# Prompt attention: the scores of two heads as products of 64 rows on the two halves of TensorE, with queries of both heads in one tile

## The chip, the cores and the metric

The kernel runs on one core of a Trainium2 chip. The metric is the device time of one execution in microseconds (us), the median of several runs. One further execution was recorded by the hardware profiler; all rows below come from it.

## The reference, cut to what matters

The program is one step of a two-layer decoder trunk: a gated DeltaNet layer, then a layer of dilated window attention, each with a feed-forward block, over a prompt of 1024 rows and 64 decode rows. The change lies in the prompt's attention of the second layer. There are 3 head groups of 16 heads of 64 channels, and 4 K/V heads, each shared by 4 query heads of a group. For every group (window, dilation) in (128, 1), (512, 4), (2048, 16) the reference does, on blocks of 128 queries against at most 256 keys:

```python
qr = residues(q).reshape(b, dil, nb, B_BLOCK, nkv, qpk, dh)
kw = key_windows(k)
vw = key_windows(v)
bias = -slope[:, :, None, None] * (dil * delta).astype(np.float32)
scores = jnp.einsum('brnqgpd,brnkgd->brngpqk', qr, kw, preferred_element_type=jnp.float32) * (dh ** -0.5) + bias
scores = jnp.where(valid[:, None, None], scores, -jnp.inf)
lse = jax.nn.logsumexp(scores, axis=-1)
probs = jnp.exp(scores - lse[..., None])
out = jnp.einsum('brngpqk,brnkgd->brnqgpd', probs, vw.astype(jnp.float32))
```

The queries are `h @ w_q`, and all of it is wanted in float32.

## The kernel before

All large products are made of float32 values split in two parts that TensorE takes in its one-pass form of float32 (`F32R` in the code): a high part, and a low part that holds the rest. A full product is then hi·hi + lo·hi + hi·lo.

The attention of the prompt runs over 24 units: 4 K/V heads, 3 groups, 2 pairs of heads. `attn_prompt` lets three kinds of generators take turns (`merge`): `q_proj` makes the queries of the next unit, `attend` works on the current one, and `combine` merges the groups of a K/V head that is done. The tile scheduler of the language sets the final order on each engine; between engines there are only semaphores, and each engine takes its instructions in order.

`q_proj` (L1366) is 72 products a unit: 3 chunks of 384, 352 and 352 rows, each 8 slices of the model by 3 parts. A chunk is then taken out of its PSUM bank (L1376, L1377). For each of the two heads of the unit ScalarE writes the high part, scaled, to partitions 0 to 63 of the head's own tile `qs[a]`, and VectorE the low part to partitions 64 to 127 of the same tile. So a column of `qs[a]` is hi over lo, and the K tiles `kh` and `kl` hold the 64 channels of K twice, on both halves of the partitions.

`attend` pushes 8 blocks a unit through a pipeline of five stages, one push a block. `scores` makes the scores of a block; two stages later `flip` turns the probabilities (transposes on TensorE, L1470, taken out by ScalarE, L1473, and VectorE, L1474), and two later `outputs` multiplies them with V (L1489) and, every second block, takes the result out (L1506 on ScalarE, L1504 on VectorE).

The scores of a block are 4 products of 128 rows (L1451). For each head `qs[a]` is multiplied with `kh`, which gives hi·kh + lo·kh at once, and then with `kl`. Both heads lie in one PSUM bank. VectorE then adds the bias and finds the maximum, an operation a head (L1455), and ScalarE takes the exponential (L1457). A block has 256 keys, or 128 at the edge of a residue class and in the whole third group.

The 8 PSUM banks of the stage are dealt out by `self.banks(mm=2, sc=2, tr=2, o=2)`: two each for `q_proj`, the scores, the transposes and the outputs.

Of the kernel before, what the change touches and what calls it, by code (L numbers as in the profile page):

```python
# [13 lines left out]
F32 = mybir.dt.float32  # L14
F32R = mybir.dt.float32r
BF16 = mybir.dt.bfloat16
AF = mybir.ActivationFunctionType
ALU = mybir.AluOpType
# [4 lines left out]
P = 128  # L23
D = 1024
KD = D // P
SP = 1024
# [38 lines left out]
def stream(*stages):  # L65

    live = [None] * len(stages)

    def push(item):
        live.insert(0, None if item is None else [item, None])  # L70
        live.pop()
        for s, x in zip(stages, live):
            if x is not None:
                x[1] = s(x[0], x[1])
            yield
    return push
# [1175 lines left out]
G = 3  # L1252
# [3 lines left out]
SLOPE = [[2.0 ** (-8.0 * (g * 16 + h + 1) / 48) for h in range(16)] for g in range(G)]  # L1256
# [25 lines left out]
class Attn:  # L1282
# [37 lines left out]
    def attn_prompt(self, ap, bp, h, w_q, kv, qd, st, oT):  # L1320

        nc = self.nc
        dist = bp.tile([P, G, 256], F32, name="dist", bufs=1)
        for g, d in ((0, 1), (1, 4)):
            nc.gpsimd.iota(dist[:, g], pattern=[[d, 256]], base=-d * P, channel_multiplier=-d, allow_small_or_imprecise_dtypes=True)
            nc.gpsimd.affine_select(out=dist[:, g], in_=dist[:, g], pattern=[[-1, 256]], base=P, channel_multiplier=1,
                                    compare_op=ALU.is_ge, fill=-FAR)
            nc.gpsimd.affine_select(out=dist[:, g], in_=dist[:, g], pattern=[[1, 256]], base=0, channel_multiplier=-1,
                                    compare_op=ALU.is_ge, fill=-FAR)
        d2 = dist[:, 2, :P]  # L1330
        nc.gpsimd.iota(d2, pattern=[[16, P]], base=0, channel_multiplier=-16, allow_small_or_imprecise_dtypes=True)
        nc.gpsimd.affine_select(out=d2, in_=d2, pattern=[[-1, P]], base=0, channel_multiplier=1, compare_op=ALU.is_ge, fill=-FAR)
        nc.gpsimd.affine_select(out=d2.rearrange("p (c i) -> p c i", c=2), in_=d2.rearrange("p (c i) -> p c i", c=2),
                                pattern=[[64, 2], [0, 64]], base=63, channel_multiplier=-1, compare_op=ALU.is_ge, fill=-FAR)
        units = [(kv_, g, pr) for kv_ in range(NKV) for g in range(G) for pr in range(2)]
        v = {"spread": (ap.tile([P, 4, DH], F32R, name="cheads", bufs=1), ap.tile([P, 8], F32, name="cblk", bufs=1), ap.tile([P, G, P], F32R, name="cws", bufs=1))}
        n = len(units)
        push = stream(*(partial(f, ap=ap, bp=bp, v=v, st=st) for f in (self.scores, self.rest, self.flip, self.rest, self.outputs)))
        for i in range(n + 2):
            ts = []  # L1340
            if i < n:
                ts.append(self.q_proj(units[i], bp, v, h, w_q, qd))
            if i == 2:
                self.spread_rows(ap, *v["spread"])
            if 0 < i <= n:
                ts.append(self.attend(units[i - 1], push, bp, v, kv, dist, i == n))
            if i > 1 and i % 6 == 1:
                last = self.combine(units[i - 2][0], ap, v, oT, st)
                ts += [last] if i < n else []
            merge(*ts)  # L1350
        return last

    def q_proj(self, u, bp, v, h, w_q, qd):
        nc = self.nc
        kv_, g, pr = u
        hi, lo = h[:2]
        col = g * 1024 + (kv_ * 4 + pr * 2) * DH
        w = self.wtile(w_q[:, col:col + P].rearrange("(k p) c -> p k c", p=P), [P, KD, P], gain=self.gain[:, 4], eng=nc.gpsimd)
        d = DIL[g]
        qs = [bp.tile([P, SP], F32R, tag=f"qs{a}", name="qs") for a in range(2)]  # L1360
        for n0, n in CHUNKS:
            ps = self.bank("mm")
            i = 0
            for k in range(KD):
                for a, b in ((w[0], hi), (w[0], lo), (w[1], hi)):
                    nc.tensor.matmul(ps[:, :n], a[:, k, :], b[:, k, n0:n0 + n], start=i == 0, stop=i == 23)  # L1366
                    i += 1
                yield 1 / 24
            a1 = min(n0 + n, SP) - n0
            for a in range(2):  # L1370
                src = ps[64 * a:64 * a + 64, :a1].rearrange("p (i r) -> p i r", r=d)

                def dst(rows):
                    return qs[a][rows].rearrange("p (r i) -> p i r", r=d)[:, n0 // d:(n0 + a1) // d, :]
                c = 0.125 / SLOPE[g][kv_ * 4 + pr * 2 + a]
                nc.scalar.activation(dst(slice(0, 64)), src, AF.Copy, scale=c)  # L1376
                nc.vector.scalar_tensor_tensor(dst(slice(64, 128)), src, c, dst(slice(0, 64)), op0=ALU.mult, op1=ALU.subtract)  # L1377
            if n0 + n > SP:
                t = bp.tile([P, SD], F32, name="qdt")
                nc.scalar.activation(t, ps[:, a1:n], AF.Copy, scale=0.125)  # L1380
                at = ((g * NKV + kv_) * 2 + pr) * SD
                nc.sync.dma_start(qd[:, at:at + SD], t)
        v[u] = qs
# [57 lines left out]
    def scores(self, i, _, ap, bp, v, st):  # L1441

        nc = self.nc
        ((kv_, g, pr), qs, (kh, kl, vh), dist, stat), b = i
        kb, nk = self.span(g, b)
        n = nk * P
        bo = P if (nk == 1 and g < 2) else 0
        ps = self.bank("sc").rearrange("p (a k) -> p a k", a=2)
        for a in range(2):
            for j, k in enumerate((kh, kl)):  # L1450
                nc.tensor.matmul(ps[:, a, :n], qs[a][:, b * P:(b + 1) * P], k[:, kb * P:kb * P + n], start=j == 0, stop=j == 1)  # L1451
        s = bp.tile([P, 2, 256], F32, name="s", bufs=4)
        for a in range(2):
            m = stat[:, 0, a, b:b + 1]
            nc.vector.tensor_tensor_reduce(out=s[:, a, :n], in0=ps[:, a, :n], in1=dist[:, g, bo:bo + n], scale=-SLOPE[g][kv_ * 4 + pr * 2 + a],  # L1455
                                           scalar=FAR, op0=ALU.add, op1=ALU.min, accum_out=m)
            nc.scalar.activation(s[:, a, :n], s[:, a, :n], AF.Exp, bias=m, scale=-1.0, accum_out=stat[:, 1, a, b:b + 1])  # L1457
        return s
# [262 lines left out]
class Trunk(Net, Gdn, Attn):  # L1721
    def run(self, a, dbias, outs):
# [63 lines left out]
        with ExitStack() as eh:  # L1786
            h2 = []
            with ExitStack() as ef:
                self.fast = []
                self.fast_pool(ef)  # L1790
                with em as es:
                    mixer = self.mixer_out(self.mixer_pool(es), mw, oT, (0, 1), x0, x1, fast((0, 2)), late=True)
                    next(mixer)
                    self.weights(es, 3, 1)
                    self.banks(mm=4, sm=4)
                    merge(mixer)
                with ExitStack() as es:
                    self.fast_pool(ef)
                    self.banks(mm=6, sm=2)
                    self.ffn_in(a["ffn_w_in"][0], gs, gd)  # L1800
            kv = dram("kv", [T, NKV, 3, DH])
            qd = dram("qd", [P, G * NKV * 2 * SD])
            flat = lambda t: t.rearrange("b t k d -> (b t) (k d)")
            kv_outs = [flat(t) for t in (kcp, vcp, kcs, vcs)]
            def after():
                self.h_pool(eh, side="right")

                def proj(es):
                    self.wpool, self.wb = self.pool(es, "ffkv"), 4
                    self.banks(mm=6, sm=2)  # L1810
                    w = self.kv_weights(a["b_w_kv"])
                    return lambda tt: self.kv_proj(tt, h2, w, kv, kv_outs)
                return into(None, h2), proj
            self.ffn_out(gs, gd, a["ffn_w_out"][0], (0, 3), x1, x2, after)
            ea, ed = ExitStack(), ExitStack()
            ap = ea.enter_context(tc.tile_pool(name="att", bufs=2, reuse_waits="tile"))
            with ExitStack() as es:
                self.weights(es, 2, 2)
                bp = es.enter_context(tc.tile_pool(name="unit", bufs=2, reuse_waits="tile"))
                self.banks(mm=2, sc=2, tr=2, o=2)  # L1820
                rest = self.attn_prompt(ap, bp, h2, a["b_w_q"][0], kv, qd, dram("st", [NKV, G, 4, 2, SP]), oT)
        with ea:
            decode = self.attn_decode(ed, kv, qd, a["cache_k"], a["cache_v"], dbias, oT)
# [58 lines left out]
```

## Time and profile before

| | |
|---|---|
| median of 3 runs | 3306.21 us (3305.95 to 3306.49) |
| profiled execution | 3316.33 us |
| its span in the profile | 3314.6 us |
| TensorE busy | 3101.6 us, 94% |
| VectorE, ScalarE, GpSimd busy | 2154.9, 1527.0, 1354.0 us (65, 46, 41%) |
| granted TensorE clock over the span | 0.967 of full |
| first and last product of `q_proj` | 1708.4 and 2299.7 us |

In the profile PE is a matmul on TensorE and PEld the load of the weights that it multiplies with; each product has one of each. Matmuls overlap in the rows, since each is shown with its way through the array: the time from one start to the next tells the rate, the duration of a row doesn't. PEld rows show when a load begins, and the time between two such starts is what a load takes when loads stand close together. DVE is VectorE, ACT ScalarE, POOL GpSimd. "128\*128" in a row is rows by columns of the weights, the next figures are what moves through them; plain float32 takes two instructions a product, the one-pass form one.

### The profile page before, as it was taken

The numbers are of one execution on the slowest core, as the hardware profiler recorded it, in microseconds if no ns is written. First come the engines' busy times: TensorE is split into PE (matmuls) and PEld (weight loads), VectorE is DVE, ScalarE is ACT, GpSimd is POOL, SyncE is SP. The second block draws the span as 40 slices with busy tenths as digits, with TensorE's granted clock in tenths as the row PEclk, the third lists the DMA queues.
The fourth block names the chain that finished last, engine by engine and source line by source line (L and its number), as shares of the span: only waits on it lengthen the run. The fifth ranks groups of instructions, "written<-read, shape, count | busy, mean of one in ns | idle before, by whom it ended". The sixth has DMA issues, their size and how long they took to land. (4 is left out here: it accounts for less than half of the span.)

```text
span 3314.6 us, 54654 instructions
## 1 busy us (share of the span) xinstructions
PE 3101.6 (94%) x20072; PEld 2841.4 (86%) x20072; DVE 2154.9 (65%) x4483; ACT 1527.0 (46%) x3739; POOL 1354.0 (41%) x1374
## 2 busy tenths in 40 slices
PE   7899999999999999999999999998898999999997
PEld 7888888888789999987788988888586999998785
DVE  5676676633666666566847777677746666665766
ACT  5444455433533333244547676767334333332344
POOL 3233333333456666544531223130114566664543
PEclk9999999999999999999999999999889999999998
DMA  4333333345322222363451111111443122224534
GB/s 136 95 109 101 101 101 101 103 130 172 124 73 90 98 98 91 130 200 86 140 164 47 33 54 53 35 54 52 156 130 118 65 98 98 97 96 151 168 104 131
DMA packets 283752, 346.42 MB, mean 105 GB/s; under 512 B 43330, under 2 KB 218802, under 8 KB 280668
## 3 DMA queue, kind: packets, MB, share of 16 engines
q1 hardware_dynamic: 271612, 293.51, 28.7%
q0 software_dynamic: 11728, 48.87, 3.8%
q8 instruction: 158, 2.59, 0.3%
q14 instruction: 110, 0.90, 0.1%
q10 hardware_dynamic: 144, 0.56, 0.0%
HBM read 245.21 MB, written 97.66 MB: 103 GB/s over the span
## 5 line engine op out<-in xcount | busy, mean ns | idle before, releaser
L784 PE MATMUL mm<-h_hi,w 128*128 128x352 f32 (+1 forms) x1536 | 444.9, 349 | 11.0 <-ACT xr L821 8.6
L451 PE MATMUL acc<-wa,ga 128*128 128x512 f32 x1716 | 418.5, 398 | 23.4 <-ACT wa L389 14.2
L451 PEld LDWEIGHTS acc<-wa,ga 128*128 128x128 f32 x1716 | 326.4, 192 | 102.8 <-ACT wa L389 15.8
L1366 PE MATMUL mm<-h_hi,w 128*128 128x352 f32 (+1 forms) x1152 | 353.8, 342 | 0.0
L784 PEld LDWEIGHTS mm<-h_hi,w 128*128 128x128 f32 x1536 | 283.6, 193 | 23.0 <-ACT xr L821 9.5
L784 PE MATMUL mm<-h_lo,w 128*128 128x352 f32 (+1 forms) x768 | 260.1, 339 | 0.0
L303 DVE TENSOR_TENSOR s<-w,s 128x512 fp32r<-128x512 f32 x132 | 190.9, 1447 | 101.8 <-ACT s L302 101.6
L302 ACT ACTIVATE s<-t 128x512 fp32r<-128x512 f32 x176 | 110.8, 630 | 301.5 <-PE mm L354 287.9
L390 DVE TENSOR_TENSOR ga<-graw,ga 128x512 fp32r<-128x512 f32 (+2 forms) x176 | 153.0, 874 | 131.0 <-ACT ga L389 130.7
L322 POOL TENSOR_TENSOR wide<-wide,v 128x288 f32<-128x288 f32 (+1 forms) x176 | 148.2, 842 | 199.5 <-DVE v L321 199.1
L389 ACT ACTIVATE ga<-graw 128x512 fp32r<-128x512 f32 (+2 forms) x176 | 100.9, 576 | 259.1 <-PE acc L451 234.4
L1457 ACT ACTIVATE s<-s,stat 128x128 f32<-128x128 f32 (+1 forms) x384 | 169.6, 443 | 95.4 <-DVE stat L1455 93.5
L1366 PEld LDWEIGHTS mm<-h_hi,w 128*128 128x128 f32 x1152 | 211.8, 189 | 1.6
L144 POOL TENSOR_TENSOR w<-raw,w 128x1024 fp32r<-128x1024 f32 x38 | 100.5, 2646 | 244.7 <-ACT w L141 162.6
L303 DVE TENSOR_TENSOR s<-t,s 128x512 fp32r<-128x512 f32 x176 | 161.7, 920 | 46.1 <-ACT s L302 45.8
L1366 PE MATMUL mm<-h_lo,w 128*128 128x352 f32 (+1 forms) x576 | 189.1, 328 | 0.0
L587 PE MATMUL mm<-mw_hi,o_hl 128*128 128x512 f32 x544 | 177.3, 403 | 3.9 <-ACT o_hl L575 3.9
L293 POOL TENSOR_TENSOR t<-w 128x512 f32<-128x512 f32 x88 | 115.2, 1311 | 146.5 <-DVE s L303 65.1
L1474 DVE TENSOR_TENSOR pl<-tr,ph 128x256 fp32r<-128x256 f32 (+1 forms) x192 | 104.6, 545 | 105.1 <-ACT ph L1473 104.0
L354 PE MATMUL mm<-b0h,s 128*128 128x256 f32 (+1 forms) x704 | 145.2, 293 | 12.2 <-ACT s L302 9.5
L831 DVE SCALAR_TENSOR_TENSOR yc<-xr,convw,yc 128x1112 f32<-128x1112 f32 x72 | 115.5, 1604 | 54.5 <-ACT yc L829 54.4
L784 PEld LDWEIGHTS mm<-h_lo,w 128*128 128x128 f32 x768 | 149.1, 194 | 1.9 <-issue 0.9
(474 smaller groups left out, 9329.4 us busy)
## 6 DMA issues: line engine op xcount, KB each, us to landing
w<-in_ffn_w_in_dram SPq DMA_DIRECT2D x88, 512.0 KB
graw<-gs SPq DMA_DIRECT2D x143, 256.0 KB
gs<-wide POOLq DMA_DIRECT2D x22, 1024.0 KB, 4.2
gs<-wide POOLq DMA_DIRECT2D x66, 256.0 KB, 2.6
raw<-in_a_w_in_dram SPq DMA_DIRECT2D x32, 512.0 KB
qkv<-f SPq DMA_DIRECT2D x24, 544.0 KB
xo<-x SPq DMA_DIRECT2D x24, 512.0 KB
raw<-in_b_w_q_dram SPq DMA_DIRECT2D x24, 512.0 KB
```

Source lines behind the costliest of these rows:

```text
L293: op(t, x, y)
L302: nc.scalar.activation(out[j][:, 0], x, AF.Copy)
L303: nc.vector.tensor_sub(out[j][:, 1], x, out[j][:, 0])
L322: nc.gpsimd.tensor_tensor(out, out, v, op=ALU.mult)
L354: nc.tensor.matmul(ps[:, :HC[c][1]], u, v, start=z == 0, stop=z == 11)
L390: nc.vector.tensor_sub(t[:, 1, :n], x, t[:, 0, :n])
L451: nc.tensor.matmul(acc[i], g[:, u, c], w[:, v], start=p == 0 and n == 0, stop=p == NP - 1 and n == 2)
L587: nc.tensor.matmul(ps, a, b[:, k], start=k == 0 and i == 0, stop=k == KD - 1 and i == len(seq) - 1)
L784: nc.tensor.matmul(ps[:, :n], a[:, k, :], b[:, k, n0:n0 + n], start=i_ == 0, stop=i_ == 23)
L831: nc.vector.scalar_tensor_tensor(yc, xr[:, j:j + CW], w(j), yc, op0=ALU.mult, op1=ALU.add)
L1366: nc.tensor.matmul(ps[:, :n], a[:, k, :], b[:, k, n0:n0 + n], start=i == 0, stop=i == 23)
L1457: nc.scalar.activation(s[:, a, :n], s[:, a, :n], AF.Exp, bias=m, scale=-1.0, accum_out=stat[:, 1, a, b:b + 1])
```

## The change

Three things change. `q_proj` takes a chunk out with one ScalarE and one VectorE operation of 128 partitions for both heads, in place of two each of 64: the pair's tile `qs` has the two heads on the two halves of its partitions, and hi and lo beside each other on the free axis. The scale, which differs by head, becomes a column of a small tile `over` that 48 memsets fill. The scores of a block become 6 products of 64 rows, 3 for each head, alternating between the halves; the first head uses TensorE's rows 0 to 63 and the second rows 64 to 127, and each head has a PSUM bank to itself. The banks are dealt out anew: 3 for the scores and 1 for the outputs.

```diff
+        v["over"] = bp.tile([P, n], F32, name="over", bufs=1)
+        for i, (kv_, g, pr) in enumerate(units):
+            for a in range(2):
+                nc.gpsimd.memset(v["over"][64 * a:64 * a + 64, i:i + 1], 0.125 / SLOPE[g][kv_ * 4 + pr * 2 + a])
...
-        qs = [bp.tile([P, SP], F32R, tag=f"qs{a}", name="qs") for a in range(2)]
+        qs = bp.tile([P, 2, SP], F32R, name="qs")
+        c = v["over"][:, ((kv_ * G + g) * 2 + pr):][:, :1]
...
-            for a in range(2):
-                src = ps[64 * a:64 * a + 64, :a1].rearrange("p (i r) -> p i r", r=d)
-
-                def dst(rows):
-                    return qs[a][rows].rearrange("p (r i) -> p i r", r=d)[:, n0 // d:(n0 + a1) // d, :]
-                c = 0.125 / SLOPE[g][kv_ * 4 + pr * 2 + a]
-                nc.scalar.activation(dst(slice(0, 64)), src, AF.Copy, scale=c)
-                nc.vector.scalar_tensor_tensor(dst(slice(64, 128)), src, c, dst(slice(0, 64)), op0=ALU.mult, op1=ALU.subtract)
+            src = ps[:, :a1].rearrange("p (i r) -> p i r", r=d)
+            hi, lo = (qs[:, x].rearrange("p (r i) -> p i r", r=d)[:, n0 // d:(n0 + a1) // d, :] for x in range(2))
+            nc.scalar.activation(hi, src, AF.Copy, scale=c)
+            nc.vector.scalar_tensor_tensor(lo, src, c, hi, op0=ALU.mult, op1=ALU.subtract)
...
-        ps = self.bank("sc").rearrange("p (a k) -> p a k", a=2)
-        for a in range(2):
-            for j, k in enumerate((kh, kl)):
-                nc.tensor.matmul(ps[:, a, :n], qs[a][:, b * P:(b + 1) * P], k[:, kb * P:kb * P + n], start=j == 0, stop=j == 1)
+        ps = [self.bank("sc") for _ in range(2)]
+        for j, (x, k) in enumerate(((0, kh), (1, kh), (0, kl))):
+            for a in range(2):
+                rows = slice(64 * a, 64 * a + 64)
+                nc.tensor.matmul(ps[a][:, :n], qs[rows, x, b * P:(b + 1) * P], k[rows, kb * P:kb * P + n], start=j == 0, stop=j == 2)
...
-            nc.vector.tensor_tensor_reduce(out=s[:, a, :n], in0=ps[:, a, :n], in1=dist[:, g, bo:bo + n], scale=-SLOPE[g][kv_ * 4 + pr * 2 + a],
+            nc.vector.tensor_tensor_reduce(out=s[:, a, :n], in0=ps[a][:, :n], in1=dist[:, g, bo:bo + n], scale=-SLOPE[g][kv_ * 4 + pr * 2 + a],
...
-                self.banks(mm=2, sc=2, tr=2, o=2)
+                self.banks(mm=2, sc=3, tr=2, o=1)
```

The product lo·kl, which the 128-row form carried along, is not made any more. The lines move: L1366 becomes L1371, L1451 becomes L1453, L1470 becomes L1472, L1489 becomes L1491, L1377 becomes L1378, L1455 becomes L1457.

How the products of one block stand in TensorE's order before, between the products of `q_proj` (mm; sc is the scores' bank, tr the transposes'):

```order
L1366 MATMUL mm<-h_hi,w 128x352
L1366 MATMUL mm<-h_lo,w 128x352
L1366 MATMUL mm<-h_hi,w 128x352
L1451 MATMUL sc<-kh,qs 128x128
L1451 MATMUL sc<-kl,qs 128x128
L1451 MATMUL sc<-kh,qs 128x128
L1451 MATMUL sc<-kl,qs 128x128
L1366 MATMUL mm<-h_hi,w 128x352
```

And in the change, at a block of 256 keys:

```order
L1371 MATMUL mm<-h_hi,w 128x352
L1371 MATMUL mm<-h_lo,w 128x352
L1371 MATMUL mm<-h_hi,w 128x352
L1453 MATMUL sc<-kh,qs 128x256 x4
L1453 MATMUL sc<-kl,qs 128x256 x2
L1371 MATMUL mm<-h_hi,w 128x352
```

Four products with `kh` and two with `kl` stand where two and two stood, and products of 128 rows are their neighbours on both sides. The 1152 products stand in 207 unbroken runs, 168 of which are the 6 products of one block in alternation. In some 15 blocks the scheduler has put other work between the two heads, as here on TensorE in the change (o is the outputs' bank):

```order
L1453 MATMUL sc<-kh,qs 128x256 x2
L1453 MATMUL sc<-kl,qs 128x256
L1472 MATMUL tr<-ident,s 128x128 x4
L1371 MATMUL mm<-h_hi,w 128x384
L1491 MATMUL o<-ph,vh 64x256
L1491 MATMUL o<-pl,vh 64x256
L1491 MATMUL o<-ph,vh 64x256
L1453 MATMUL sc<-kh,qs 128x256 x2
L1453 MATMUL sc<-kl,qs 128x256
```

There the three products of the first head come first, and those of the second only after transposes and outputs of earlier blocks.

On VectorE a chunk of queries before, with the maxima (L1455) and the low parts of the probabilities (L1474) that are queued around it:

```order
L1377 SCALAR_TENSOR_TENSOR qs<-mm,qs 64x88x4
L1504 COPY og<-o 64x256
L1455 ISA s,stat<-sc,dist 128x256
L1455 ISA stat 128x1
L1377 SCALAR_TENSOR_TENSOR qs<-mm,qs 64x88x4
L1455 ISA s,stat<-sc,dist 128x256
```

And in the change:

```order
L1476 TENSOR_TENSOR pl<-tr,ph 128x512
L1378 SCALAR_TENSOR_TENSOR qs<-mm,over,qs 128x88x4
L1506 COPY og<-o 64x256
L1513 COPY srow<-tr 32x128
L1405 TENSOR_TENSOR vh<-kvt,vh 128x8x64
L1457 ISA s,stat<-sc,dist 128x128
```

One operation of 128 partitions stands where two of 64 stood, with nothing of the scores between.

## Rows read from the trace of the kernel before

**Rows 1.** The profile page: busy us, share of the span and instructions of each engine.

```profile
PE 3101.6 (94%) x20072; PEld 2841.4 (86%) x20072; DVE 2154.9 (65%) x4483; ACT 1527.0 (46%) x3739; POOL 1354.0 (41%) x1374
```

**Rows 2.** Windows over the attention: us, busy by engine, clock, DMA share, GB/s.

```profile
2300.00:2318.00 18.00, 12.73 (x93) 11.42 (x91) 14.57 (x71) 14.49 (x56) 2.66 (x1) 0.91 0.58 187
sum 610.00, PE 572.93 PEld 543.46 DVE 438.04 ACT 433.01 POOL 124.32; mean PE 114.59 PEld 108.69 DVE 87.61 ACT 86.60 POOL 24.86
```

**Rows 3.** Groups of lines, 1708 to 2318 us: busy, mean ns, idle before, releaser.

```profile
L1474 DVE TENSOR_TENSOR pl<-tr,ph 128x256 fp32r<-128x256 f32 (+1 forms) x188 | 103.0, 548 | 105.0 <-ACT ph L1473 104.0
L1377 DVE SCALAR_TENSOR_TENSOR qs<-mm,qs 64x384 fp32r<-64x384 f32 (+1 forms) x144 | 98.2, 682 | 42.6 <-ACT qs L1376 38.4
L1504 DVE COPY og<-o 64x256 f32<-64x256 f32 x93 | 50.0, 537 | 10.1 <-ACT og L1506 8.8
...
L1376 ACT ACTIVATE qs<-mm 64x384 fp32r<-64x384 f32 (+1 forms) x144 | 96.1, 667 | 38.2 <-PE mm L1366 19.3 <-DVE qs L1377 17.9
...
L1506 ACT ACTIVATE og<-o 64x256 f32<-64x256 f32 x93 | 50.2, 540 | 0.1
```

**Rows 4.** Waits, 1708 to 2318 us: us in total, times, longest.

```profile
PE sc L1451 <- DVE stat L1455: 12.3, 13, 2.1
PE tr L1410 <- DVE pl L1474: 10.8, 4, 2.7
```

**Rows 5.** Timeline of PE at a block of 128 keys: start, us, engine, line.

```profile
2000.90 0.22 PE L1451 MATMUL sc<-kh,qs 128*128 128x128 f32 x1
2000.96 0.28 PE L1451 MATMUL sc<-kl,qs 128*128 128x128 f32 x1
2001.07 0.28 PE L1451 MATMUL sc<-kh,qs 128*128 128x128 f32 x1
2001.18 0.28 PE L1451 MATMUL sc<-kl,qs 128*128 128x128 f32 x1
2001.30 0.39 PE L1366 MATMUL mm<-h_hi,w 128*128 128x384 f32 x1
```

**Rows 6.** Timeline of PE: the end of an outputs product, and a block of 256 keys.

```profile
1871.89 0.28 PE L1489 MATMUL o<-ph,vh 128*64 128x256 f32 x1
1872.00 0.33 PE L1366 MATMUL mm<-h_hi,w 128*128 128x352 f32 x1
...
1872.49 0.29 PE L1451 MATMUL sc<-kh,qs 128*128 128x256 f32 x1
...
1872.98 0.32 PE L1366 MATMUL mm<-h_hi,w 128*128 128x352 f32 x1
```

**Rows 7.** Timeline of PE around a product of 64 rows in the DeltaNet stage.

```profile
198.96 0.32 PE L784 MATMUL mm<-h_hi,w 128*128 128x352 f32 x1
199.21 1.12 PE L1175 MATMUL C<-um,kdec 64*128 64x512 f32 x2
200.26 0.43 PE L784 MATMUL mm<-h_hi,w 128*128 128x352 f32 x1
```

**Rows 8.** Timeline of PEld there, with the idle time before a load in brackets.

```profile
198.80 0.19 PEld L784 LDWEIGHTS mm<-h_hi,w 128*128 128x128 f32 x1
199.21 0.29 PEld L1175 LDWEIGHTS C<-um,kdec 64*128 64x128 f32 x2 [0.22 <-DVE r L1188]
200.26 0.19 PEld L784 LDWEIGHTS mm<-h_hi,w 128*128 128x128 f32 x1 [0.76 <-issue]
200.37 0.19 PEld L784 LDWEIGHTS mm<-h_lo,w 128*128 128x128 f32 x1
```

**Rows 9.** Line L1175: matmul durations (min, median, max in ns).

```profile
L1175 PE MATMUL C<-um,kdec x32: 589/641/693, 193.9 to 752.1; 64*128 64x512 f32 x32
```

**Rows 10.** Line L1451: first and last start, and forms with counts.

```profile
L1451 PE MATMUL sc<-kh,qs x384: 218/278/561, 1723.0 to 2317.3; 128*128 128x128 f32 x104, 128*128 128x256 f32 x88
```

**Rows 11.** POOL: a group of small memsets, and the timeline at the start of the stage.

```profile
L815 POOL MEMSET xr<- 128x3 f32 x24 | 2.4, 99 | 19.8 <-DVE yc L831 19.8
...
1721.95 2.38 POOL L144 TENSOR_TENSOR w<-raw,w 128x1024 fp32r<-128x1024 f32 x1 [14.15 <-PE tr L1410]
```

More of the change, by code (lines that the diff above doesn't have):

```diff
@@ L1355, in q_proj @@
         kv_, g, pr = u
-        hi, lo = h[:2]
+        h_hi, h_lo = h[:2]
         col = g * 1024 + (kv_ * 4 + pr * 2) * DH
@@ L1364, in q_proj @@
             for k in range(KD):
-                for a, b in ((w[0], hi), (w[0], lo), (w[1], hi)):
+                for a, b in ((w[0], h_hi), (w[0], h_lo), (w[1], h_hi)):
                     nc.tensor.matmul(ps[:, :n], a[:, k, :], b[:, k, n0:n0 + n], start=i == 0, stop=i == 23)
```

## Prediction

> **What bounds the kernel now.** The page comes first: TensorE is busy for 94% of the span, and no other engine comes near [rows 1]. Then the stretch that the change touches, 1708 to 2318 us: of 610 us TensorE shows 573 busy, 37 idle, and 5.3 of these 37 lie in the last 18 us, where no queries are made any more [rows 2]. So in the attention a microsecond more on TensorE is a microsecond more of time, except where it falls into these 37 us.
>
> The second view is that of the groups of lines and waits, since VectorE and ScalarE are nearly as full: VectorE is busy for 438 us [rows 2], and it stands still for another 104 before the low parts of the probabilities and 38 before those of the queries, each time for ScalarE [rows 3]. That is 580 of 610 us. Here the two engines hand work to and fro, and TensorE waits for them a little: 12.3 us before scores, for the maxima that free the scores' bank, and 10.8 us before the transposes of K, for a bank that L1474 frees [rows 4]. The third view is the timeline of single products; the sum rests on that.
>
> **The products of a block.** Before, 4 products of 128 rows. At 128 keys they take from 2000.90 to 2001.30, 0.40 us, and after the first they follow each other at 0.11 us, though 128 columns pass in 0.06 (the first gap) [rows 5]: the loads set the pace, and loads that stand close together start 0.11 us apart [rows 8]. At 256 keys the 4 take from 1872.49 to 1872.98, 0.49 us or 0.12 each [rows 6]. There are 104 blocks of 128 keys and 88 of 256 [rows 10], whose forms are counted once a block: 104 x 0.40 + 88 x 0.49 = 85 us.
>
> After, 6 products of 64 rows, two heads in turn on two halves of the rows. If both halves load and multiply at the same time, a block is 3 rounds. At 128 keys that is two rounds at the load's pace and a last one of 0.06: 0.28 us; at 256 keys 3 x 0.12, say 0.35. Sum: 104 x 0.28 + 88 x 0.35 = 60 us, 25 us **saved**. If instead only one load goes on at a time, five more loads follow the first, 5 x 0.11 plus the last product's 0.06 or 0.12: 0.61 and 0.67 us, 122 us in all, 37 us **lost**. No row shows products on two halves of the rows in turn, so these are the two bounds. The nearest rows are loads of whole tiles, which do come one after the other, but a tile of 128 rows uses all rows and says nothing on two halves; I take the 60 us, on the guess that a load of 64 rows holds up only its own half. The Trainium skill, "TensorEngine Tiling (Array Packing)", section Key Properties, states that different tiles can execute loads and products in parallel; by it the sum would be the 60 us, by the spacing of the loads alone 122. Whether this trace agrees can't be seen, as it has no such pair.
>
> **The change of shape.** The 6 products stand between products of 128 rows on both sides. The DeltaNet stage has the same step: L1175, two passes of plain float32 on 64 rows by 128 columns, between products of L784 on 128 rows [rows 7, 8]. The last load of L784 starts at 198.80 and its product at 198.96: a load goes ahead while the product before it runs, and a product of 352 columns takes 0.16. So the load of L1175 could start at 198.96. It starts at 199.21, which is 0.09 us after that product is through (198.96 + 0.16 = 199.12), and then the load itself lies open, 0.11. Together 0.20 us to go in. Going out: the row of both passes lasts 1.12 and the second pass alone 0.59 [rows 9], so it starts 0.53 after the first; that is a load of 0.11 and 0.42 of columns. The second is through at 199.21 + 0.53 + 0.42 = 200.16; the next load starts at 200.26, with 0.76 us of idle before it that nothing explains ("issue"), and again lies open: 0.10 + 0.11. The two changes cost 0.41 us. The gap on the way in is put down to VectorE, but the one on the way out, of the same size, has no releaser [rows 8]; so I read both as TensorE running empty when the number of rows changes. Its place in the sum: 207 unbroken runs of 64-row products x 0.41 = **85 us more**. Below, the cost could be smaller where TensorE waits anyway (part of the 37 us).
>
> The same page and section of the Trainium skill says that changing the tiling mode drains TensorE, and that speaks against this change. The rows above agree for rows, at 0.09 to 0.10 us each way. They don't for columns: L1489, with 64 columns of weights, starts at 1871.89 and the product of 128 columns behind it at 1872.00, 0.11 later, no more than a load takes [rows 6]. If columns drained it too, the kernel before would pay that at each L1489; so I charge rows alone.
>
> **The waits.** What the queries cost halves: 72 of 144 operations on VectorE at 682 ns, 49 us, and 72 of 144 on ScalarE at 667 ns, 48 us [rows 3], together with their to and fro (38 and 18 us). For 128 partitions I take the same duration as for 64, as L1474 moves 128 partitions in 548 ns. None of this lies on TensorE; it makes VectorE and ScalarE come sooner to the maxima and to L1474. At best all idle time of TensorE goes: 37 us less. Against it stand the banks. With 3 banks, the second head of a block gets the bank of the first head of the block just before, so its product waits for that maximum and no longer for one a block earlier; where the two blocks stand close, TensorE waits, and all of `q_proj` behind it. With a single outputs' bank, the first product of a pair of blocks waits until L1506 and L1504 have taken the pair before out, two times 0.54 us at best [rows 3]. I bound it by a doubling of the 12.3 us, and by a quarter of the 96 pairs waiting 1.08 us, 26: together 38 us more. Between -37 and +38 I take **0**: the relief and the new waits sit on the same engines, and a TensorE that comes 2.5 us a unit later finds both further on.
>
> **Costed at nothing.** The 48 memsets are 48 x 0.10 = 4.8 us on POOL [rows 11], which stands idle for 14 us before its next split of weights at 1721.95; without that cover the first chunk of queries would be late by 4.8 us, once. SP's DMAs are the same.
>
> **Sum.** -25 + 85 + 0 = **+60 us**. From the profiled execution's 3316.3 us that is 3376; it is 10.1 us above the median of 3306.2, and I carry the difference to the median: **3366 us**. With the waits' bounds the likeliest case spans 3329 to 3404.
>
> **Rivals.**
> 1. One load at a time: the two heads don't run together, and the change doesn't do what it is laid out for. +37 + 85 = +122, 3428 us (3391 to 3466 with the waits). For it: all loads of the trace come one after the other. Against it: none of them is of another half. Chance 0.28.
> 2. No emptying between shapes for one-pass float32. L1175 is plain float32, so this isn't excluded by a row. Then 25 us are saved, and with 23 us of TensorE's two waits for VectorE gone the time is 3306 - 48 = 3258 us. The point of decision is 25 / 207 = 0.12 us a run: below that the products alone win. Against it: the two ways in and out cost the same kind of gap although what follows is one-pass and what precedes too. Chance 0.08.
> 3. The banks bind: heads do run together, but the waits for maxima and outputs exceed 38 us, for instance 24 units x 3 us; +60 + 72 = +132, 3438 us. For it: VectorE is occupied or waiting for 580 of 610 us now. Against it: it loses 49 us of work. Chance 0.08.
> 4. The extra time is swallowed. All 37 us of idle would have to go, no new wait to come, and the change of shape to cost 0.30 us rather than 0.41 (207 x 0.11 = 23): then +60 - 37 - 23 = 0, 3306 us. Chance 0.05.
>
> My forecast has the remaining 0.51. A measurement of this kernel can tell 0.2%, 6.6 us, from no change; faster by more than that is rival 2, 0.08; within it rival 4, 0.05; slower all the rest, 0.87. The range for 8 in 10 reaches from below the likeliest case, 3312, to 3450, which takes in most of rival 1 and of rival 3.
>
> **What would show it.** Right: in the timeline each run of L1453 has an idle load before and behind it, of about 0.2 us, pairs of L1453 starts closer than 0.11 us, the stretch of the attention longer by 50 to 80 us and all stages after it unchanged in length; L1378 with 72 operations at the old duration. Rival 1: six starts of L1453 0.11 us apart. Rival 2: a load of L1453 that starts with the product before it. Rival 3: waits "sc <- DVE stat" or "o <- DVE og" of tens of us on TensorE. I am wrong if the attention gets shorter, or if the time moves elsewhere.

## The result and the profile after

The change takes 3349.97 us, median of 4 runs (3347.70 to 3354.07), against 3306.24 (3305.95 to 3306.49): a ratio of 1.0131, 95% interval 1.0113 to 1.0148, 44 us slower (37 to 49). The profiled execution took 3354.07 us, its span is 3352.4, 37.8 longer than before.

| us from the span's start | before | after |
|---|---|---|
| first product of `q_proj` | 1708.4 | 1705.1 |
| last product of the scores | 2317.6 | 2361.0 |
| between them (the stage) | 609.1 | 655.9 (+46.8) |
| from there to the end | 997.1 | 991.4 |

So the time is lost in the attention alone. The page's row of engines: TensorE has 384 products and 54.5 us of busy time more, VectorE and ScalarE have 72 instructions and 42.8 and 37.5 us less [rows 1].

```profile
PE 3156.1 (94%) x20456; PEld 2838.2 (85%) x20456; DVE 2112.1 (63%) x4411; ACT 1489.5 (44%) x3667; POOL 1360.7 (41%) x1422
```

The timeline of PE at a block of 128 keys, and that of PEld for the same block; they answer to [rows 5, 8]. "x4" merges four products or loads of one form, and the time in front is the first one's start.

```profile
1999.87 0.28 PE L1491 MATMUL o<-ph,vh 128*64 128x256 f32 x1
2000.08 0.44 PE L1453 MATMUL sc<-kh,qs 64*128 64x128 f32 x4
2000.35 0.27 PE L1453 MATMUL sc<-kl,qs 64*128 64x128 f32 x2
2000.56 0.43 PE L1371 MATMUL mm<-h_hi,w 128*128 128x352 f32 x1
2000.83 0.32 PE L1371 MATMUL mm<-h_lo,w 128*128 128x352 f32 x1
```

```profile
1999.76 0.13 PEld L1491 LDWEIGHTS o<-ph,vh 128*64 128x64 f32 x1
2000.08 0.30 PEld L1453 LDWEIGHTS sc<-kh,qs 64*128 64x128 f32 x4 [0.18 <-issue]
2000.29 0.19 PEld L1453 LDWEIGHTS sc<-kl,qs 64*128 64x128 f32 x2
2000.56 0.19 PEld L1371 LDWEIGHTS mm<-h_hi,w 128*128 128x128 f32 x1
2000.66 0.19 PEld L1371 LDWEIGHTS mm<-h_lo,w 128*128 128x128 f32 x1
```

Two things are to be read here. The first four loads and the next two stand 0.21 us apart (2000.08 to 2000.29): two rounds of 0.11 us, of two loads each. Six loads one after the other would need 0.55 from the first start to the last. In the single records behind these rows the two heads' loads start 3 ns apart, and their products too: **the halves run together**. And the load of L1453 does not start while the product before it runs, as loads of 128 rows do: L1491 begins at 1999.87 and has 256 columns, 0.11 us, so it is through at 1999.98, and the load starts at 2000.08, 0.10 later. Behind the run the same: the third round's load starts at 2000.29, takes 0.11, its columns 0.05, so it is through at 2000.45; the next load starts at 2000.56, and then lies open until 2000.66. Over all 207 runs, the idle time before loads of L1453 that nothing explains is

```profile
  issue: 32.9, 153
```

us and times: some 0.21 a time. From the end of the columns before a run to the first column behind it, an unbroken block now takes 0.69 us at 128 keys and 0.77 at 256 (medians of 100 and 71), where it took 0.41 and 0.49.

TensorE's waits in the stage (us in total, times, longest), to [rows 4]:

```profile
PE o L1491 <- DVE og L1506: 15.4, 17, 1.3
...
PE tr L1411 <- DVE pl L1476: 1.5, 4, 0.4
...
PE sc L1453 <- DVE stat L1457: 0.2, 1, 0.2
```

The waits for the maxima (12.3) and before the transposes of K (10.8) are gone; a wait for the single outputs' bank has come, 15.4. The queries' evictions in the groups of lines, to [rows 3]:

```profile
L1377 ACT ACTIVATE qs<-mm,over 128x384 fp32r<-128x384 f32 (+2 forms) x72 | 55.0, 764 | 35.9 <-PE mm L1371 34.4
L1378 DVE SCALAR_TENSOR_TENSOR qs<-mm,over,qs 128x384 fp32r<-128x384 f32 (+2 forms) x72 | 53.9, 749 | 45.8 <-ACT qs L1377 44.4
```

Half as many, 764 ns each on ScalarE and 749 on VectorE instead of 667 and 682. The 128 partitions are not what is dearer: with a constant as scale they take 666 and 700 (run 5 below), and 64 partitions with the scale from a column take 759 and 752 (run 6). Last, windows over the end of the stage (columns as in [rows 2]; the clock is the third figure from the end):

```profile
2185.00:2300.00 115.00, 111.60 (x777) 95.60 (x776) 74.69 (x231) 68.37 (x206) 26.91 (x19) 0.99 0.12 35
2300.00:2352.00 52.00, 49.13 (x337) 40.92 (x335) 29.80 (x117) 32.27 (x108) 2.66 (x1) 0.90 0.25 75
2352.00:2361.00 9.00, 8.01 (x39) 5.67 (x39) 8.47 (x46) 4.50 (x17) 0.00 (x0) 0.50 0.50 133
```

The granted clock is 0.50, the level of 1.2 GHz, in the last 9 us. The 0.90 of the 52 us before them is a mean of both levels (full is 2.4 GHz): the 16 us from 2336 on alone have 0.68, so the clock fell some 10 us earlier, after the last product of `q_proj` at 2336.8. In windows of 10 us over the whole stage, the time missing to the full clock is 16.4 us, before 3.4.

**The ledger of the stage.** With every kind of run at its median, the scores' products and their ways in and out take 155.0 us, before 89.1: +65.9. The clock, with all the missing time taken as lost: +13.0. The rest of +46.8 is -32. It is a remainder and not measured by itself; I take it as less waiting. The rows show a part of it: the idle time of TensorE in the stage falls from 37 to 23 us.

### The profile page after: what moved, and what is told of

Same layout as the page of the kernel before. It is cut to its first block, busy times and chain, and to the rows that moved or that the text cites. A ratio compares the mean times of both kernels' runs of the same rounds, so it can differ in the third digit from the quotient of the medians.

```text
span 3352.4 us, 55311 instructions
## 1 busy us (share of the span) xinstructions
PE 3156.1 (94%) x20456; PEld 2838.2 (85%) x20456; DVE 2112.1 (63%) x4411; ACT 1489.5 (44%) x3667; POOL 1360.7 (41%) x1422
## 5 line engine op out<-in xcount | busy, mean ns | idle before, releaser
L784 PE MATMUL mm<-h_hi,w 128*128 128x352 f32 (+1 forms) x1536 | 442.2, 347 | 10.4 <-ACT xr L821 7.8
L1371 PE MATMUL mm<-h_hi,w 128*128 128x352 f32 (+1 forms) x1152 | 369.3, 352 | 0.0
L1371 PEld LDWEIGHTS mm<-h_hi,w 128*128 128x128 f32 x1152 | 213.0, 189 | 14.7
L1371 PE MATMUL mm<-h_lo,w 128*128 128x352 f32 (+1 forms) x576 | 190.9, 331 | 0.0
L1491 PE MATMUL o<-ph,vh 128*64 128x256 f32 x560 | 139.2, 296 | 15.4 <-DVE og L1506 15.4
```

The lines of the kernel that those rows point to most:

```text
L1491: nc.tensor.matmul(po[:64, b % 2], w, x, start=j == 0, stop=j == len(seq) - 1)
```

## The experiments

Ratios are to the kernel before, run beside each; 0.0010 is 3.3 us. "Over the change" compares with its 1.0131.

**1. Products of two blocks in one run (`pairs`).** Every second block makes the scores of two blocks, side by side in the same two banks.

```diff
+        if b % 2 == 0:
+            v["sc"] = [self.bank("sc") for _ in range(2)]
+            for e in (b, b + 1):
+                kb, nk = self.span(g, e)
+                n, c0 = nk * P, e % 2 * 256
...
+                        nc.tensor.matmul(v["sc"][a][:, c0:c0 + n], qs[rows, x, e * P:(e + 1) * P], k[rows, kb * P:kb * P + n], start=j == 0, stop=j == 2)
...
+        ps = [y[:, b % 2 * 256:b % 2 * 256 + 256] for y in v["sc"]]
```

> The change, with the products of two blocks (12 of them) in one run; each head's bank holds both blocks. 109 runs instead of 207. Theory (a run of 64-row products costs 0.41 us for going in and out of the shape, whatever its length): 98 x 0.41 = 40 us less than the change, 3310 us, give or take 10 for waits, since maxima come a block later at the earliest. Rival (the loss lies in the products themselves, which would not overlap well, or in waits for banks): no more than 10 us less, 3340 us or above.

Measured: 3318.84 us, ratio 1.0030 (1.0018 to 1.0042), 33 us less than the change, inside the theory's 40 give or take 10. The timeline shows what went: two blocks between one way in and one way out.

```profile
1851.87 0.32 PE L1371 MATMUL mm<-h_hi,w 128*128 128x352 f32 x1
1852.12 0.44 PE L1454 MATMUL sc<-kh,qs 64*128 64x128 f32 x4
1852.40 0.27 PE L1454 MATMUL sc<-kl,qs 64*128 64x128 f32 x2
1852.51 0.39 PE L1454 MATMUL sc<-kh,qs 64*128 64x128 f32 x4
1852.73 0.28 PE L1454 MATMUL sc<-kl,qs 64*128 64x128 f32 x2
1852.94 0.43 PE L1371 MATMUL mm<-h_hi,w 128*128 128x352 f32 x1
```

109 runs instead of 207, so 33 / 98 = 0.34 us a run at the end of the program. The products are the same; the price is by the run.

**2. One head after the other (`in_order`).** The loops over `a` and over the three parts change places, so that a block's order is three products of the first half of the rows, then three of the second.

```diff
-        for j, (x, k) in enumerate(((0, kh), (1, kh), (0, kl))):
-            for a in range(2):
+        for a in range(2):
+            for j, (x, k) in enumerate(((0, kh), (1, kh), (0, kl))):
```

> The change, with the 3 products of the first head before the 3 of the second instead of in turn; banks, evictions and the number of runs (203) as in the change. Theory (in turn the halves load and multiply at the same time, one after the other they follow the load's pace of 0.11 us): a block of 128 keys 0.61 instead of 0.28 us, one of 256 keys 0.67 instead of 0.35, 62 us more than the change, 3412 us. Rival (the halves gain nothing from taking turns, or loads of the second half run ahead anyway): within 10 us of the change.

Measured: 3352.89 us, ratio 1.0130 (1.0112 to 1.0147): no difference to the change. The theory failed and the rival held; PEld's timeline tells why:

```profile
1852.09 0.30 PEld L1453 LDWEIGHTS sc<-kh,qs 64*128 64x128 f32 x4 [0.25 <-issue]
1852.31 0.20 PEld L1453 LDWEIGHTS sc<-kl,qs 64*128 64x128 f32 x2
1852.58 0.19 PEld L1371 LDWEIGHTS mm<-h_hi,w 128*128 128x128 f32 x1
```

Again four loads with `kh` and only then two with `kl`, though in the program a `kl` stands third. In the single records the first product of the second head starts 0.01 us after the first of the first head, and 0.15 before the first head's second. The scheduler has not put them in turn: in the built program, 168 of the 203 runs on TensorE's queue are three products of the first half and then three of the second. So this run could not serialize the heads, and it says nothing on the price of that; it shows that the alternation in the code isn't what makes them run together.

**3 and 4. One product more in the kernel before.** At the head of each of the 104 blocks of 128 keys, into columns that nothing reads, with 64 rows (`one_more_of_64`) or with 128 as a control (`one_more_of_128`).

```diff
+        if nk == 1:
+            nc.tensor.matmul(ps[:, 0, P:], qs[0][:64, b * P:(b + 1) * P], kh[:64, kb * P:kb * P + P], start=True, stop=True)
```

> The kernel before with one product more at the head of each of the 104 blocks of 128 keys: 64 rows (the high parts of the first head's queries and kh), 128 columns, into columns of the scores' bank that nothing reads. Theory (TensorE empties when the number of rows changes, 0.41 us in and out): 104 x (0.41 + 0.05 for its own columns) = 48 us more, less up to 13 us that idle time swallows, so 3341 to 3354 where before has 3306. Rival (what the change pays is the pairing of the halves, its products or its waits, and a lone product of 64 rows costs no more than one of 128): 104 x 0.11 = 11 us more, 3317. In the trace the theory wants the load of the added product to start only after the product of q_proj before it is through, and the load after it likewise.

> The control to the run before: the same added product at the same place, but with all 128 rows. Theory and rival alike: 104 x 0.11 us at the pace of the loads = 11 us more, about 3317, less what idle time swallows. The theory wants the difference to the run with 64 rows to be 104 x 0.35 to 0.41 = 36 to 43 us, less some idle; the rival wants no difference.

Measured: ratio 1.0089 (1.0070 to 1.0108), 29 us more, with 64 rows; 1.0078 (1.0052 to 1.0104), 26 us more, with 128. PE's timeline with 64 rows:

```profile
2001.27 0.32 PE L1366 MATMUL mm<-h_hi,w 128*128 128x352 f32 x1
2001.53 0.32 PE L1450 MATMUL sc<-kh,qs 64*128 64x128 f32 x1
2001.78 0.33 PE L1453 MATMUL sc<-kh,qs 128*128 128x128 f32 x1
2001.94 0.28 PE L1453 MATMUL sc<-kl,qs 128*128 128x128 f32 x1
```

On TensorE the theory's price is there to the hundredth: with its ways in and out a block takes 0.86 us (median) instead of 0.41, so 0.45 for the added product; the control's takes 0.52, 0.11 for it. But the two programs end 3 us apart and not 35, so both expectations missed. What makes them equal stands in TensorE's waits, of the run with 64 rows

```profile
PE sc L1450 <- DVE stat L1457: 12.6, 16, 1.3
```

and of the control:

```profile
PE sc L1450 <- DVE stat L1457: 23.4, 18, 2.0
```

Where TensorE is faster, it waits longer for the maxima. In the kernel before it isn't alone on the path, and a price read on TensorE can't be carried to the end one to one. The control costs 26 us and not the 11 that it holds TensorE. This wait is 11 us longer in it than before, and 12 us are missing to the full clock in its stage, before 3.4; together that is enough, but what set off either isn't shown. Runs 10 and 11 repeat the pair where TensorE hardly waits.

**5. Merged evictions alone (`merged_evictions`).** The kernel before, with the queries taken out by one operation of 128 partitions on each engine. It leaves out the second head's scale, and its products take the tiles of high and of low parts as they lie, so its scores are other numbers; the number and shape of its products are those of before.

```diff
-            for a in range(2):
-                src = ps[64 * a:64 * a + 64, :a1].rearrange("p (i r) -> p i r", r=d)
...
+            src = ps[:, :a1].rearrange("p (i r) -> p i r", r=d)
+            hi, lo = (y.rearrange("p (r i) -> p i r", r=d)[:, n0 // d:(n0 + a1) // d, :] for y in qs)
```

> The kernel before, with one eviction of 128 partitions a chunk on ScalarE and on VectorE. The tiles hold the high parts of both heads in one and the low parts in the other, and the scores multiply them as they are, so the scores are other numbers; the count and shape of products are those of before. Theory (half of the queries' evictions gone relieves the waits of TensorE for VectorE): 15 to 30 us less than before, 3276 to 3291 us. Rival (those waits don't hang on the queries): within 6 us of before.

Measured: 3278.63 us, ratio 0.9912 (0.9884 to 0.9939), 29 us less than before. The wait for the maxima falls from 12.3 to

```profile
PE sc L1448 <- DVE stat L1452: 4.6, 8, 0.7
```

**6. The evictions undone in the change (`split_evictions`).**

```diff
-            nc.scalar.activation(hi, src, AF.Copy, scale=c)
-            nc.vector.scalar_tensor_tensor(lo, src, c, hi, op0=ALU.mult, op1=ALU.subtract)
+            for a in range(2):
+                r = slice(64 * a, 64 * a + 64)
+                nc.scalar.activation(hi[r], src[r], AF.Copy, scale=c[r])
+                nc.vector.scalar_tensor_tensor(lo[r], src[r], c[r], hi[r], op0=ALU.mult, op1=ALU.subtract)
```

> The change with only the removal of the queries from PSUM undone: again two operations of 64 partitions on ScalarE and two on VectorE a chunk, each with its head's part of the scale column; the products of 64 rows and the banks stay. Theory (the relief of VectorE and ScalarE is worth in the change about what it was worth in the kernel before, 29 us): 15 to 30 us more than the change, 3365 to 3380. Rival (TensorE is longer busy in the change, so that the two engines have room and the relief is worth little): within 6 us of the change, 3344 to 3356. In the waits the theory wants TensorE's waits for the maxima or for the transposes' bank to come back to over 10 us.

Measured: 3401.32 us, ratio 1.0280 (1.0255 to 1.0305), 49 us over the change: more than theory or rival gave it. It is not the exact reverse of run 5, since the scale still comes from a column: 759 and 752 ns an operation, where the kernel before has 667 and 682. Windows over its stage:

```profile
1700.00:2000.00 300.00, 282.33 (x1910) 244.58 (x1909) 186.15 (x544) 194.71 (x532) 56.10 (x76) 0.97 0.16 45
2000.00:2250.00 250.00, 233.41 (x1553) 199.30 (x1553) 158.78 (x484) 162.35 (x464) 47.33 (x29) 0.95 0.14 39
```

The clock is 0.97 and 0.95 where the change has 0.99. In windows of 10 us, 37.3 us are missing to the full clock, against 16.4 in the change: up to 21 of the 49 us are clock. TensorE stood still more, 46 us of idle time in this stage, 23 in that of the change; but that this made the clock fall isn't shown, as the kernel before has 37 us of idle time and only 3.4 missing. The other 28 us, or more, are near what run 5 gave; which waits they are was not settled (for the outputs' bank 21.1 us, before the transposes of K 9.7, for the maxima 5.4, together 19 more than in the change).

**7. The banks alone (`one_output_bank`).** The kernel before with `sc=3, o=1`.

```diff
-                self.banks(mm=2, sc=2, tr=2, o=2)
+                self.banks(mm=2, sc=3, tr=2, o=1)
```

> The kernel before, with 3 banks for the scores and 1 for the outputs. Theory (the single outputs' bank makes TensorE wait until both evictions of the pair of blocks before are done; in the change it waits for it some 15 us in the products' rows and 20 in the loads'): 15 to 40 us more than before, 3321 to 3346 us. Rival (the third scores' bank pays for it, or the waits only move): within 6 us of before.

Measured: 3313.22 us, ratio 1.0023 (1.0002 to 1.0043), 8 us more: less than the theory's 15 to 40, and hardly beyond the rival's 6. A new wait comes, and that for the maxima goes, so they mostly trade places:

```profile
PE o L1489 <- DVE og L1504: 30.3, 26, 2.1
```

**8. The banks undone in the change (`banks_two_two`).** The same line, back to 2 and 2.

> The change with the banks dealt out as before: 2 for the scores (one a head) and 2 for the outputs. Theory (the change's one outputs' bank costs what it cost in the kernel before, 7 us, or the 15 to 20 us of waits for og that its trace shows, and two banks for scores are enough as each block's maxima come soon): 5 to 15 us less than the change, 3335 to 3345. Rival (with two banks each block's scores wait for the maxima of the block just before): 10 us or more over the change, 3360 or more, with waits of sc for stat over 20 us.

Measured: 3354.15 us, ratio 1.0143 (1.0127 to 1.0158), 4 us over the change, which the intervals don't tell from none. The 15.4 us for the outputs' bank are gone, and

```profile
PE sc L1453 <- DVE stat L1457: 18.2, 21, 1.3
```

stands in their place. Neither expectation held: one bank too few costs about the same on either side.

**9. The same change without a change of shape (`block_diagonal`).** K is kept block-diagonally, so a product of 128 rows makes both heads at once. Queries and evictions are those of the change. K has one pair of tiles, filled by halves as the last block that reads a half is through. The banks are those of the kernel before, which by run 8 makes no difference that could be told in the change.

```diff
+                nc.scalar.activation(kh[r, a, s], ps[r], AF.Copy)
+                nc.vector.tensor_sub(kl[r, a, s], ps[r], kh[r, a, s])
...
-        ps = [self.bank("sc") for _ in range(2)]
+        ps = self.bank("sc").rearrange("p (a k) -> p a k", a=2)
         for j, (x, k) in enumerate(((0, kh), (1, kh), (0, kl))):
-            for a in range(2):
-                rows = slice(64 * a, 64 * a + 64)
-                nc.tensor.matmul(ps[a][:, :n], qs[rows, x, b * P:(b + 1) * P], k[rows, kb * P:kb * P + n], start=j == 0, stop=j == 2)
+            nc.tensor.matmul(ps[:, :, :n], qs[:, x, b * P:(b + 1) * P], k[:, :, kb * P:kb * P + n], start=j == 0, stop=j == 2)
...
-                self.banks(mm=2, sc=3, tr=2, o=1)
+                self.banks(mm=2, sc=2, tr=2, o=2)
```

> The change with its scores made in another form, all products of 128 rows: K stands block-diagonally (the first head's K over zeros, then zeros over the second head's K, beside each other on the free axis), so that one product gives both heads in one bank; 3 products a block (hi kh, lo kh, hi kl) of 256 or 512 columns, the same parts as in the change. Queries leave PSUM as in the change, banks as before (2, 2). K is kept in one tile instead of two in turn, filled by halves, with 24 more operations each on ScalarE and VectorE, 0.5 to 0.8 us. Theory (the change of shape is what the change pays): 104 x 0.33 + 88 x 0.64 = 91 us of products against 85 before, no emptying; with 29 us of relief, of which the 24 operations take some 7 to 10 back: 3306 + 6 - 20 = 3292, 3280 to 3305, faster than both. Rival (what costs is having both heads' queries in one tile, one wait for both, and six thirds of products instead of four): not below 3330.

Measured: 3291.51 us, ratio 0.9948 (0.9930 to 0.9966): 17 us **faster than before**, 61 faster than the change, as the theory had it. PE's timeline at a block of 128 keys has no gaps:

```profile
2000.12 0.28 PE L1500 MATMUL o<-ph,vh 128*64 128x256 f32 x1
2000.24 0.40 PE L1462 MATMUL sc<-kdh,qs 128*128 128x256 f32 x2
2000.48 0.28 PE L1462 MATMUL sc<-kdl,qs 128*128 128x256 f32 x1
2000.60 0.28 PE L1500 MATMUL o<-ph,vh 128*64 128x256 f32 x1
```

A block takes 0.37 us at 128 keys (before 0.41) and 0.71 at 256 (before 0.49): there the doubled columns are the dearer part. The clock is 1.00 through the whole stage.

**10 and 11. The added product again, in the block-diagonal form (`diagonal_and_64`, `diagonal_and_128`).** The edit is that of runs 3 and 4.

> The block-diagonal form with one product more at the head of each of the 104 blocks of 128 keys: 64 rows, 128 columns, into columns of the scores' bank that nothing reads. In the kernel before, the same addition held TensorE for 0.45 us a block in the timeline, and the control with 128 rows for 0.11, but the two ended within some us of each other, since TensorE's waits shrank. Theory (the price is the emptying, and in the kernel before it is partly swallowed because TensorE waits there for VectorE): here TensorE waits least (13.5 us idle), so the addition costs 104 x 0.45 = 47 us, less up to 10 of idle: 37 to 47 over block_diagonal, 3328 to 3340. Rival (the emptying is swallowed in any case and the end is set by VectorE and ScalarE): under 25 us more, 3316 or less.

> The control to the run before: the same added product with 128 rows, in the block-diagonal form. Theory: 104 x 0.11 = 11 us over block_diagonal, 3297 to 3308, and 25 to 36 us less than with 64 rows. Rival (end set by VectorE and ScalarE, or the order that the scheduler finds decides): within 12 us of the run with 64 rows.

Measured: ratios 1.0061 (1.0042 to 1.0081) and 0.9970 (0.9959 to 0.9981): 37 and 7 us over run 9. Here the two lie 30 us apart, 0.29 a block, where the timeline has 0.82 against 0.48 (medians). PE's timeline with 64 rows

```profile
2000.92 0.34 PE L1375 MATMUL mm<-h_hi,w 128*128 128x384 f32 x1
2001.19 0.33 PE L1462 MATMUL sc<-kdh,qs 64*128 64x128 f32 x1
2001.45 0.51 PE L1464 MATMUL sc<-kdh,qs 128*128 128x256 f32 x2
```

and with 128:

```profile
2001.53 0.30 PE L1462 MATMUL sc<-kdh,qs 128*128 128x128 f32 x1
2001.68 0.45 PE L1464 MATMUL sc<-kdh,qs 128*128 128x256 f32 x2
```

The clock is full through the stage in both, as in run 9, so it has no part in the difference. So the emptying is paid in time once TensorE has no other waits that could shrink.

**12. K put in place by GpSimd (`diagonal_by_gpsimd`).** Run 9 with K taken out by one operation of 128 partitions per engine, and 96 copies on GpSimd.

```diff
+            nc.scalar.activation(t2[:, 0], ps, AF.Copy)
+            nc.vector.tensor_sub(t2[:, 1], ps, t2[:, 0])
...
+                    nc.gpsimd.tensor_copy(y[r, a, s], t2[r, x])
```

> The block-diagonal form with K's halves taken out by one operation of 128 partitions each on ScalarE and VectorE, as in the kernel before, and put in place by 96 copies of 64 partitions on GpSimd, which is busy for 134 of 590 us there. Theory (the 24 + 24 operations of 0.6 to 0.7 us that the block-diagonal form adds on the two engines hold TensorE up a little): 3 to 10 us less than block_diagonal, 3282 to 3289. Rival (GpSimd's copies stand in the way of K, or nothing waits for those operations): 3290 to 3310, with TensorE's waits for K (sc for kd) above 3 us if the copies are late.

Measured: 3298.81 us, ratio 0.9969 (0.9956 to 0.9981), 7 us over run 9, which the intervals hardly tell from none; the theory's 3 to 10 us less did not come. In its profile the stage is 4 us shorter, 582.1 us against 585.7, but what follows is 9 us longer, 1015.6 against 1006.9. The decode attention, which follows, now waits for its cache:

```profile
PE tr L1676 <- DMA kc<-in_cache_k_dram: 7.9, 3, 5.5
```

SP issues the first of these transfers at 2299.0, 10 us after the last product of the scores; in run 9 it did so at 2277.0, 11 us before it. What the attention gains is given back right behind it, and run 9 remains the fastest form that was tried.

## Why the prediction was right, and where its terms were off

The forecast was 3366 us, slower with 0.87; it is 3350, inside the likeliest case's own 3329 to 3404. Step by step:

- **What bounds the kernel**: only partly so. "A microsecond more on TensorE is a microsecond more of time" with 37 us as the margin was too simple. Runs 3 and 4 added 47 and 11 us of TensorE time and cost 29 and 26. In the block-diagonal form, where VectorE and ScalarE are relieved, the same additions cost 37 and 7.
- **The products, -25**: the choice held. Heads run together, a round is 0.11 us at 128 keys, and rival 1 falls. At 256 keys a round is 0.11 to 0.12 as well.
- **The change of shape, +85**: the mechanism held, with the size that was read off one product of plain float32. The load waits until 0.10 us after the product before it is through, lies open for 0.11, and the same again on the way out: 0.41 us, and with the 0.05 of its own columns about the 0.45 of run 3. Run 1 shows that it is paid by the run, and the pairs 3 and 4, 10 and 11 that it hangs on the number of rows. Rival 2 falls. The two terms together came to +66 instead of +60; blocks whose two heads were parted by other work are the dearest, 0.80 us for each half at 256 keys. The Trainium skill, "TensorEngine Tiling (Array Packing)", section Key Properties, says that a change of mode drains TensorE and that tiles run in parallel; both agree with these rows, and the gap behind the drain is here 0.10 us, and 0.21 with the load that it leaves open. A change of the columns alone has no such gap: in run 9 L1500, with 64 columns, and L1462, with 128, follow each other at 0.12 us.
- **The waits, 0 between -37 and +38**: this is the term that was mis-sized. By the ledger's remainder the waiting fell by 32 us, near the lower bound. The prediction had set new waits for the banks equal to the relief of the evictions. Alone, in the kernel before, the relief is worth 29 us (run 5) and the banks cost 8 (run 7); in the change, undoing the evictions costs 49, up to 21 of it clock (run 6), and undoing the banks saves nothing (run 8). Rival 3 was a real wait, 15.4 us, but the waits would have had to exceed 38.
- **The clock, not in the sum**: up to +13 us, from one profile of each kernel. As the stage runs out, without products of `q_proj` between the scores, the granted clock falls to 0.50 and stays there for the last 9 us; before, the last 18 us had 0.91 [rows 2]. The profiles of runs 1, 2 and 8, with the same products, miss 15.5, 10.6 and 12.1 us in the stage, so it is no single accident.
- **Where it appears**: the stage is longer by 47 us and nothing behind it is, as forecast; "50 to 80" was too high by the waits. Two other signs came out otherwise: L1378 takes 749 ns and not the old 682, and behind a run the rows of the loads show hardly any idle time, so the 0.10 us there is read from the starts.

So +60 was in truth +66 +13 -32 = +47 in the stage. In the profiled executions the parts ahead of it and behind it are 3 and 6 us shorter, which makes 38; by the medians it is 44. That the emptying is the cause is shown by run 9 (the same queries, evictions of queries and parts of the product, without 64-row products, and the time is under that of before) and by runs 10 and 11, where the same product costs 30 us more with 64 rows than with 128. That the total is off by only 16 us is in part luck: the clock, which the sum didn't have, took back a part of what the waits gave.

## What to carry to other kernels

Small products on halves of the rows can pay only if they come in long runs: count the unbroken runs in the final order, and charge 0.4 us for each time TensorE goes from 128 rows to 64 and back. Here the products of a block save 0.12 us (0.28 against 0.40 at 128 keys), so by this estimate a run would have to hold four blocks; the longest tried, two, still was slower than before (run 1). Where two heads shall share TensorE, a block-diagonal operand keeps the number of rows; it doubles the columns, so against the form of before it wins where the loads set the pace (0.37 against 0.41 us at 128 keys) and loses where the columns do (0.71 against 0.49 at 256). And try the parts of a change alone: the merged evictions inside this slower kernel were worth 29 us by themselves, and a price read on one engine is paid in full only when the others don't wait.

## What was not expected of the hardware

- TensorE doesn't keep the program's order between products on different halves of its rows (run 2: the second head's first product, fourth in the program, starts 0.15 us ahead of the second in the program). That each engine takes its instructions in order, as it stands above, is too strong for such pairs. The Trainium skill, "TensorE: Matmul & The Clock Gate", section The mechanism, says that matmuls start and end strictly in the program's order; the starts of this trace differ from that for two halves of the rows.
- The clock can be a large part of a difference. With the evictions split again, the granted clock falls to 0.95 over 250 us, and up to 21 of 49 us are lost that way; in the block-diagonal form it stays at 1.00. Idle time alone doesn't tell which: the kernel before idles for 37 us in the stage and misses 3.4 us of clock, the change idles for 23 and misses 16.4. What makes it fall stays open.
- Going from 128 rows to 64 and back costs nearly the same for one product of 64 rows as for six or twelve: 0.10 + 0.11 us in and 0.10 + 0.11 out, 0.40 to 0.43 in the medians of run 3, the change and run 1.
